# Six homes for the gathered expert rows, a gate matrix loaded in four pieces, and a re-dealt opening, in a two-layer block with 16,384 experts

## The chip, the cores and the metric

One core of one Trainium2 chip runs the whole program. The metric is the device time of one execution in microseconds (us); lower is better. The engines are named as the profile names them: PE (TensorE matmul), PEld (its weight load), DVE (VectorE), ACT (ScalarE), POOL (GpSimd) and SP (SyncE, which here only issues DMAs). The profile's granted clock is a share of the 2.4 GHz level; the other level is 1.2 GHz.

## What is computed

Two layers over 512 tokens (256 of `x`, 256 of `ctx`), width 1024. Each layer has a mixing half (a Hyena convolution whose filters come from a small sine network, a Fourier mix and differential attention) and a PEER half, in which each token takes 128 (8 heads of 16) of 16,384 experts. All of it is float32; only `x` of the last layer is returned. The parts that the change touches:

```python
def rms_norm(x, g):
    return x * lax.rsqrt(jnp.mean(x * x, axis=-1, keepdims=True) + EPS) * g
def modulate(x, g, shift, scale):
    return rms_norm(x, g) * (1 + scale) + shift

def hyena_kernels(L, w1, b1, freq, w2, b2, w3):      # does not depend on x
    h = jnp.sin(freq * (feats @ w1 + b1))
    h = jnp.sin(freq * (h @ w2 + b2))
    h = (h @ w3).reshape(L, 2, HY_ORDER, HY_WIDTH) * decay
    k = jnp.concatenate([h[:, 0], 0, h[:0:-1, 1]], axis=0)
    return jnp.fft.rfft(k / jnp.sum(jnp.abs(k), axis=0, keepdims=True), axis=0)

def peer(t, wq, keys, u, v):
    ...                                              # scores, top-k: idx, g  [T, 128]
    hid = jnp.einsum('td,tkd->tk', tc, u[ic])
    return jnp.einsum('tk,tkd->td', gc * gelu(hid), v[ic])
...
# per layer: shift, scale, gate, ... = silu(c) @ w_ada + b_ada   (6 x 1024 numbers per stream)
# mixing reads modulate(x, g_mix, shift, scale); PEER reads modulate of the result
```

## The kernel before

**Number form.** Matmuls are done as three float32r products: `split` (L106 on ACT, L110 on DVE) cuts a tile into a high part (`wh`, `vh`, `ah`) and the rest (`wl`, `vl`, `al`), and PE forms high*high, high*low, low*high (`mm`, L98; `mm3`). A weight chunk is 512 KB, loaded by `wraw` (L138 to L140) into the ring `w4` of six buffers. The instructions are put into an order for each engine by a scheduler, which follows the priorities of program order; `pin` keeps the marked DVE instructions in their written order.

**The opening** (`ada_first`, layer 0 only). `modulate` needs shift and scale of layer 0. For each of eight steps, one chunk of `w_ada` (a shift column block) is multiplied with `silu(c)` on DVE, two `scalar_tensor_tensor` (STT) with a sum into `mods` (L171) and one add of the bias each (L175); one chunk of `w_ada1` (rows of the scale matrix) goes through PE into two PSUM banks. In between `x` is loaded in four parts, squared on ACT, its squares are added on POOL (`tot`, L217), summed over partitions on PE, turned into 1/rms (`rs`, L220 and L221), and POOL multiplies `x` by `rs` (L200). At the end the scale row is transposed on PE (the small matmuls after L204), and `modulate` writes `nh` and `nl`, which every projection matmul (`pm<-nh,wh` ...) of phase 1 reads. Only behind `modulate` does the program write out `filters`: the sine network (tiles `sa`, `sk`), its product with the decay (`hd`), the sum of magnitudes (`ab`, L301), its reciprocal (`rn`, L305) and the transform with the matrix `fwd` into five tiles `K`. They are a generator, and a `drain` runs it at once.

**The experts.** All 16,384 experts are computed densely for 384 of layer 0's tokens: 128 blocks of 128 experts, two blocks to a superblock, so 64 superblocks in a loop. `stage1` of a block forms the hidden values `a` (1024 deep product, GELU), or for 32 blocks loads them from DRAM (`a<-Hd`, L796), where an earlier stage (`prefill`) left them. They are then multiplied by the gate matrix (`a<-a,gt`, L800, zero where a token didn't choose the expert) and split into `ah`, `al`. `stage2` of the superblock before loads its two `v` chunks (`wv`, L809, three buffers), splits them in four halves (`vh`, `vl`) and adds into six PSUM banks. The gate matrix of eight blocks (four superblocks, a *group*) is one load of 1.5 MB (`gt<-Gd`, L792). The two blocks of the first superblock of each of the 16 groups are prefilled ones. `a` has three buffers. Layer 1 runs the same loop for its 256 tokens, without the next part.

**The gathered rows.** The last 128 tokens of layer 0 don't go through the dense loop. Instead POOL fetches, for each of the 128 places k, one row of `u` for each token (`row<-in_ug_dram,ix`, L1049, 512 KB), and DVE forms its dot product with the token (L1067); four per superblock in the first 32 superblocks. In the second 32 superblocks the rows come from `v` and DVE adds them into `acc[:, 0:2]` (L1077, the first by L1075). These DVE instructions are pinned. A row tile has three buffers, so a gather waits on POOL's queue until DVE is done with the row three before it. Of `acc` (eight parts of 512 columns; the token vectors and the sum lie in the first two) parts 2 to 7 are not used in this stage.

## Time and profile before

| what | us |
| --- | --- |
| median of 3 runs | 3024.02 (3019.01 to 3027.01) |
| the profiled execution | 3018.95 |
| its span | 3017.2 |
| opening, up to the first projection matmul | 56.14 |
| phase 1 of layer 0 (with the filters) | 48.66 (56.14 to 104.80) |
| experts of layer 0 | 965 (887 to 1852) |
| experts of layer 1 | 621 (2387 to 3008) |

How to read it: the profiled execution lies 1.75 us above its own span and 5.07 us below the median. The page's busy times are means over stages with unlike limits, so the table is cut by stage: what a stage can give back is read from its waits and its granted clock. A row of a timeline gives start, duration, engine, line, operation, output<-inputs, the count where several stand in one row, and in brackets the idle time ahead of it with what ended that.

### The profile page before, as it was taken

How to read it: one execution, taken by the hardware profiler on the slowest of the kernel's cores; microseconds unless marked ns; L12 is line 12 of the kernel's file. 1: busy time of each engine (PE TensorE's matmuls, PEld its weight loads, DVE VectorE, ACT ScalarE, POOL GpSimd, SP SyncE). 2: the span in 40 equal slices, each digit the busy share in tenths (PEclk: the TensorE clock that was granted, in tenths of full speed). 3: DMA queues.
4: the chain of work that ended last, by engine and by line, in shares of the span. 5: the costliest groups of instructions: out<-in, count | busy, mean ns of one | idle time of the engine just before them, and what ended most of it. 6: DMA issues, size and time to landing. Idle time of an engine off the chain costs nothing.

```text
span 3017.2 us, 43660 instructions
## 1 busy us (share of the span) xinstructions
PE 2864.0 (95%) x15976; PEld 2435.9 (81%) x15976; DVE 2223.2 (74%) x4464; ACT 1247.6 (41%) x2294; POOL 700.7 (23%) x609
## 2 busy tenths in 40 slices
PE   6889999999989999999999999899799999999999
PEld 2678778776667888888898897788788898899888
DVE  7766786797977887888887787746688657765665
ACT  3334565421443333333333334336414455555554
POOL 4544433430013333333333332300200000000000
PEclk8899999999999999999999999999999999999999
DMA  7323555233788898889888885225457977766662
GB/s 261 108 97 116 175 180 220 101 114 105 278 332 326 315 326 300 307 318 323 312 317 300 307 312 186 81 97 176 165 162 250 331 249 243 259 223 223 221 224 103
DMA packets 234536, 682.19 MB, mean 226 GB/s; under 512 B 21956, under 2 KB 92682, under 8 KB 231120
## 3 DMA queue, kind: packets, MB, share of 16 engines
...
q8 instruction: 125, 2.05, 0.3%
...
HBM read 612.20 MB, written 67.11 MB: 225 GB/s over the span
## 4 chain that ended last, share of the span: by engine, by line
PE 52%; issue 15%; DVE 14%; DMA 13%; POOL 4%; ACT 2%; POOLq 0%; DVEq 0%; SPq 0%; ACTq 0%
PE pm L98 32%; PE pa L98 19%; DMA row<-in_ug_dram,ix 7%; DMA row<-in_v_dram,ix 4%; DVE og L734 3%; POOL row L1049 2%; DVE wl L110 1%; DVE oa L730 1%; DVE junk L171 1%; DVE acc L1077 1%; DVE junk L1067 1%; DVE vl L110 1%; POOL qt L466 0%; DMA a<-Hd 0%; POOL pr L167 0%
## 5 line engine op out<-in xcount | busy, mean ns | idle before, releaser
L98 PE MATMUL pm<-th,wh 128*128 128x256 f32 (+2 forms) x1680 | 532.4, 317 | 2.3 <-DVE th L241 2.3
L98 PE MATMUL pm<-tl,wh 128*128 128x256 f32 (+2 forms) x1680 | 530.2, 316 | 3.3 <-DVE tl L242 3.2
L98 PE MATMUL pm<-th,wl 128*128 128x256 f32 (+2 forms) x1680 | 529.7, 315 | 0.7 <-DVE wl L110 0.7
L106 ACT CAST wh<-w 128x1024 fp32r<-128x1024 f32 x328 | 343.0, 1047 | 409.3 <-PE pm L98 351.1
L110 DVE TENSOR_TENSOR wl<-w,wh 128x1024 fp32r<-128x1024 f32 x312 | 392.5, 1259 | 161.5 <-ACT wh L106 160.7
L98 PE MATMUL pa<-vl,ah 128*128 128x512 f32 x1024 | 406.1, 397 | 26.5 <-DVE vl L110 26.5
L110 DVE TENSOR_TENSOR vl<-wv,vh 128x512 fp32r<-128x512 f32 x512 | 339.1, 687 | 119.2 <-ACT vh L106 113.6
L106 ACT CAST vh<-wv 128x512 fp32r<-128x512 f32 x512 | 305.3, 619 | 265.4 <-PE pm L98 86.0
L98 PE MATMUL pa<-vh,ah 128*128 128x512 f32 x1024 | 402.5, 394 | 5.1 <-ACT vh L106 5.1
L98 PE MATMUL pa<-vh,al 128*128 128x512 f32 x1024 | 403.7, 394 | 0.3 <-DVE al L110 0.3
L98 PE MATMUL pm<-acc,w 128*128 128x256 f32 (+1 forms) x1280 | 355.6, 427 | 8.6 <-ACT acc L1011 8.6
L98 PEld LDWEIGHTS pm<-tl,wh 128*128 128x128 f32 x1680 | 320.9, 191 | 13.6 <-DVE tl L242 4.5
L98 PEld LDWEIGHTS pm<-th,wh 128*128 128x128 f32 x1680 | 321.0, 191 | 11.8 <-DVE th L241 2.9
L98 PEld LDWEIGHTS pm<-th,wl 128*128 128x128 f32 x1680 | 320.8, 191 | 5.4 <-DVE wl L110 0.9
L106 ACT CAST ah<-a 128x384 fp32r<-128x384 f32 (+1 forms) x256 | 117.7, 460 | 439.5 <-DVE a L800 399.6
L98 PEld LDWEIGHTS pm<-acc,w 128*128 128x128 f32 x1280 | 235.8, 191 | 78.0 <-ACT acc L1011 9.0
L1049 POOL DMA_INDIRECT row<-in_ug_dram,ix x128 | 165.3, 1291 | 507.7 <-DVE junk L1067 298.5
L98 PEld LDWEIGHTS pa<-vl,ah 128*128 128x128 f32 x1024 | 194.7, 190 | 70.5 <-DVE vl L110 32.7
L1049 POOL DMA_INDIRECT row<-in_v_dram,ix x128 | 170.6, 1332 | 311.5 <-DVE acc L1077 279.3
L98 PEld LDWEIGHTS pa<-vh,ah 128*128 128x128 f32 x1024 | 194.5, 190 | 44.8 <-ACT vh L106 6.3
L98 PEld LDWEIGHTS pa<-vh,al 128*128 128x128 f32 x1024 | 194.7, 190 | 41.1 <-DVE al L110 0.8
L1077 DVE SCALAR_TENSOR_TENSOR acc<-row,gg,acc 128x1024 f32<-128x1024 f32 x127 | 162.8, 1282 | 62.7 <-DMA row<-in_v_dram,ix 61.8
(309 smaller groups left out, 5292.5 us busy)
## 6 DMA issues: line engine op xcount, KB each, us to landing
w<-in_u_dram SPq DMA_DIRECT2D x256, 512.0 KB, 4.2
wv<-in_v_dram SPq DMA_DIRECT2D x256, 512.0 KB, 4.9
w<-in_w_ada_dram SPq DMA_DIRECT2D x96, 512.0 KB, 4.3
w<-in_w_in_dram SPq DMA_DIRECT2D x88, 512.0 KB, 3.8
...
w<-in_wq_dram SPq DMA_DIRECT2D x32, 512.0 KB, 3.6
...
```

What stands on the lines that cost most here:

```text
L98: T.matmul(o, l, r, start=start, stop=stop, skip_group_check=True)
L106: S.copy(hi, src)
L110: (eng or V).tensor_tensor(lo[:, ks], src[:, ks], hi[:, ks].bitcast(F32), ALU.subtract)
L171: i = V.scalar_tensor_tensor(slot((P, 1024), BF16, "junk"), w, 1.0, sil[:, s], op0=ALU.mult, op1=ALU.mult, accum_out=m)
L730: V.tensor_tensor(oa, row(0), iob, ALU.is_equal)
L734: V.tensor_tensor(og[:, w * HG:(w + 1) * HG], oa, gv[:, w * HG:(w + 1) * HG, None].to_broadcast([P, HG, P, 2]), ALU.mult)
L1049: nc.gpsimd.indirect_dma_start(out=r, out_offset=None, in_=src, in_offset=bass.IndirectOffsetOnAxis(ap=ix, axis=0))
L1067: pin(V.scalar_tensor_tensor(slot((P, 1024), BF16, "junk"), r, 1.0, ta, op0=ALU.mult, op1=ALU.mult, accum_out=hg[:, k:k + 1]))
L1077: pin(V.scalar_tensor_tensor(ta, r, gg[:, k:k + 1], ta, op0=ALU.mult, op1=ALU.add))
```

## The change

There are four parts. First, the rows with odd k are gathered into parts 2 to 7 of `acc`, three places in turn, and those with even k into the three buffers as before: six homes. Second, the gate matrix of a group is loaded in four pieces of 384 KB (three of the twelve column blocks each); the pieces of the next group are written one at a time into the even blocks of the current group, and those of the first group ahead of the loop. Third, `wv` gets four buffers in place of three, and the tiles `a`, `ah`, `al` are cut to the width that is used. Fourth, in the opening half of shift (four of eight column blocks) joins scale on PE: a step loads 1536 columns in two pieces (512 KB and 256 KB) and has three matmuls, and DVE does four chunks in place of eight. POOL's additions of squares and its multiplication by `rs` go to DVE. The generator `filters` is started ahead of the loop and moved on by one step behind every second chunk, and what is left of it, the five `K` steps, is drained behind `modulate`.

```diff
@@ -74,8 +74,8 @@
     def slot(shape=(P, 512), dt=F32, name="t"):
         return scope["sl"].tile(list(shape), dt, tag="sl", name=nm(name))
 
-    def tagged(tag, dt=F32, bufs=2):
-        return scope["ex"].tile([P, 512], dt, tag=tag, name=nm(tag), bufs=bufs)
+    def tagged(tag, dt=F32, bufs=2, n=512):
+        return scope["ex"].tile([P, n], dt, tag=tag, name=nm(tag), bufs=bufs)
 
     def b16t(shape=(P, 8, 512), dt=F32, name="b"):
         return b16.tile(list(shape), dt, tag="b16", name=nm(name))
@@ -174,7 +174,9 @@
                     pin(i)
                 V.tensor_tensor(m, m, b, ALU.add)
 
-    def ada_first(x, rs):
+    NSH = 4
+
+    def ada_first(x, rs, side):
         cT = slot((P, 8, 32), name="cT")
         V.memset(cT, 0.0)
         ct = slot((P, 8, 2), name="ct")
@@ -183,30 +185,41 @@
             nc.scalar.dma_start(sil[:, s], A["crow"][s:s + 1, :].to_broadcast([P, 1024]))
         S.activation(cT[:, :, 0:2], ct, AF.Silu)
         S.activation(sil, sil, AF.Silu)
-        ps = [pmt() for _ in range(2)]
+        next(side)
+        nb = (8 + NSH) // 4
+        ps = [pmt() for _ in range(nb)]
         tot = slot(name="tot")
         for c in range(8):
-            ada(0, c, c + 1)
-            w = wraw(A["w_ada1"][:, c])
-            for h in range(2):
-                mm(ps[h][0:32], cT[:, c], w[:, h * 512:(h + 1) * 512], c == 0, c == 7)
-            if c < 4:
-                nc.sync.dma_start(x[:, 2 * c:2 * c + 2], A["xT"][:, 2 * c:2 * c + 2])
-                for k in (2 * c, 2 * c + 1):
-                    squares(x, k, 0, NT, tot, eng=G)
-            if c == 4:
-                summed(tot, 0, NT, rs)
-                for k in range(8):
-                    G.tensor_tensor(x[:, k], x[:, k], rs, ALU.mult)
+            for a in range(0, nb * 512, 1024):
+                k = min(1024, nb * 512 - a)
+                w = w4.tile([P, 1024], F32, tag="w4", name=nm("w4"))
+                nc.sync.dma_start(w[:, :k], A["w_ada1"][:, c, a:a + k])
+                for q in range(k // 512):
+                    mm(ps[a // 512 + q][0:32], cT[:, c], w[:, q * 512:(q + 1) * 512], c == 0, c == 7)
+            if c % 2 == 0:
+                nc.sync.dma_start(x[:, c:c + 2], A["xT"][:, c:c + 2])
+                f = NSH + c // 2
+                if f < 8:
+                    ada(0, f, f + 1)
+            else:
+                for k in (c - 1, c):
+                    squares(x, k, 0, NT, tot)
+                next(side, None)
+        summed(tot, 0, NT, rs)
+        for k in range(8):
+            V.tensor_tensor(x[:, k], x[:, k], rs, ALU.mult)
         pt = pat()
-        for q in range(2):
+        for q in range(nb):
             m = slot(name="m1")
             (S.copy if q % 2 else V.tensor_copy)(m[0:32], ps[q][0:32])
             for f in range(4):
                 k = 4 * q + f
                 mm(pt[:, k * 32:(k + 1) * 32], m[0:32, f * P:(f + 1) * P], ident[0:32, 0:32], k == 0, True)
-        V.tensor_tensor(mods[:, 0, :, 8:16], pt[:, 0:256].rearrange("p (f s) -> p s f", s=32)[:, 0:2],
-                        pv(0, "b_ada")[:, None, 8:16].to_broadcast([P, 2, 8]), ALU.add)
+        p4 = pt.rearrange("p (f s) -> p s f", s=32)[:, 0:2]
+        for d, k in ((8, 0), (0, 8)):
+            w = min(8, 8 + NSH - k)
+            V.tensor_tensor(mods[:, 0, :, d:d + w], p4[:, :, k:k + w],
+                            pv(0, "b_ada")[:, None, d:d + w].to_broadcast([P, 2, w]), ALU.add)
 
     def squares(x, c, a, b, tot, new=slot, eng=None):
         if c == 0:
@@ -764,7 +777,7 @@
             for c in range(8):
                 cs = slice(c * P, (c + 1) * P)
                 mm3(ps[:, :n], uh[:, cs], ul[:, cs], th[:, c, :n], tl[:, c, :n], c == 0, c == 7)
-        a = scope["ha"].tile([P, 512], F32, tag="a", name=nm("a"))
+        a = scope["ha"].tile([P, NT - NG], F32, tag="a", name=nm("a"))
         S.activation(a[:, :n], ps[:, :n], AF.Gelu)
         return a
 
@@ -784,28 +797,37 @@
     def experts(l, n, npre, th, tl, Gd, Hd, acc, hook):
         nq = n // 32
         pacc = [pat() for _ in range(4)] + [pmt() for _ in range(n // P * 2 - 4)]
-        gt = [None]
+        gts = {}
+        pieces = 4
+
+        def gates(g, i):
+            if i == 0:
+                gts[g] = b16t((P, nq, GB, 32), name="gt")
+            qs = slice(i * nq // pieces, (i + 1) * nq // pieces)
+            nc.sync.dma_start(gts[g][:, qs], Gd[:, qs, g * GB:(g + 1) * GB, :])
+
+        for i in range(pieces):
+            gates(0, i)
 
         def stage1(b):
-            if b % GB == 0:
-                gt[0] = b16t((P, 16, GB, 32), name="gt")
-                nc.sync.dma_start(gt[0][:, :nq], Gd[:, :nq, b:b + GB, :])
+            if b % 2 == 0 and b // GB + 1 < P // GB:
+                gates(b // GB + 1, b % GB // 2)
             if b in PRE_BLOCK[l]:
                 k = PRE_BLOCK[l].index(b)
-                a = scope["ha"].tile([P, 512], F32, tag="a", name=nm("a"))
+                a = scope["ha"].tile([P, NT - NG], F32, tag="a", name=nm("a"))
                 nc.sync.dma_start(a[:, :n], Hd[k, :, :n])
             else:
                 a = hidden(l, n, b, th, tl)
             a3 = a[:, :n].rearrange("p (q k) -> p q k", k=32)
-            V.tensor_tensor(a3, a3, gt[0][:, :nq, b % GB], ALU.mult)
-            ah, al = tagged("ah", F32R, 4), tagged("al", F32R, 4)
+            V.tensor_tensor(a3, a3, gts[b // GB][:, :, b % GB], ALU.mult)
+            ah, al = tagged("ah", F32R, 4, n), tagged("al", F32R, 4, n)
             split(ah[:, :n], al[:, :n], a[:, :n])
             return ah, al
 
         def stage2(b0, blocks):
             ws = []
             for i in range(SB):
-                w = scope["ex"].tile([P, 1024], F32, tag="wv", name=nm("wv"), bufs=3)
+                w = scope["ex"].tile([P, 1024], F32, tag="wv", name=nm("wv"), bufs=4)
                 nc.sync.dma_start(w, A["v"][l, b0 + i])
                 ws.append(w)
             vs = {}
@@ -869,11 +891,13 @@
         fd = mp.tile([P, 2, P], F32, name=nm("fd"))
         rope = mp.tile([P, 2, 3, 64], F32, name=nm("rope"))
         pre = x is None
+        K = []
+        side = filters(l, fwd, K)
         if pre:
             x = b16t(name="x")
         rs = slot(name="rs")
         if pre:
-            ada_first(x, rs)
+            ada_first(x, rs, side)
         nc.gpsimd.dma_start(fwd, A["fwd"])
         nc.gpsimd.dma_start(inv, A["inv"])
         nc.gpsimd.dma_start(fd, A["fd"])
@@ -882,8 +906,7 @@
         nl = big.tile([P, 8, NT], F32R, tag="B", name=nm("nl"))
         gains(l, "g_mix", 1)
         modulate(l, x, rsl if last else None, 0, L if last else NT, 0, nh, nl)
-        K = []
-        drain(filters(l, fwd, K))
+        drain(side)
 
         br = b16t(name="br")
         vx = b16t(name="vx")
@@ -1044,8 +1067,11 @@
         drain(pf)
         pools(es, f"e{l}", ex=2, sl=1)
 
-        def rows_of(src, ix):
-            r = scope["ex"].tile([P, 1024], F32, tag="row", name=nm("row"), bufs=3)
+        def rows_of(src, ix, k):
+            if k % 2:
+                r = acc[:, 2 + k // 2 % 3 * 2:4 + k // 2 % 3 * 2].rearrange("p a b -> p (a b)")
+            else:
+                r = scope["ex"].tile([P, 1024], F32, tag="row", name=nm("row"), bufs=3)
             nc.gpsimd.indirect_dma_start(out=r, out_offset=None, in_=src,
                                          in_offset=bass.IndirectOffsetOnAxis(ap=ix, axis=0))
             return r
@@ -1063,14 +1089,14 @@
             ta = acc[:, 0:2].rearrange("p a b -> p (a b)")
             for k in range(4 * (sb % 32), 4 * (sb % 32) + 4):
                 if sb < 32:
-                    r = rows_of(A["ug"], ix[:, 0, k:k + 1])
+                    r = rows_of(A["ug"], ix[:, 0, k:k + 1], k)
                     pin(V.scalar_tensor_tensor(slot((P, 1024), BF16, "junk"), r, 1.0, ta, op0=ALU.mult,
                                                op1=ALU.mult, accum_out=hg[:, k:k + 1]))
                 else:
                     if k == 0:
                         S.activation(hg, hg, AF.Gelu)
                         V.tensor_tensor(gg, gg, hg, ALU.mult)
-                    r = rows_of(A["v"][0].rearrange("b p d -> (b p) d"), ix[:, 1, k:k + 1])
+                    r = rows_of(A["v"][0].rearrange("b p d -> (b p) d"), ix[:, 1, k:k + 1], k)
                     if k == 0:
                         V.tensor_scalar(ta, r, gg[:, k:k + 1], None, op0=ALU.mult)
                     else:
```

Two small hunks are left out: the result rows also take the ring of four `wv` buffers, and the host puts the columns of half of shift behind those of scale in `w_ada1`, which thereby holds 1536 columns.

Where the scheduler puts these instructions shows in their order on the engines. The first place is SP's queue at the start of a group of layer 0's experts, before (`w4` are `u` and `w_ada` chunks, `a<-Hd` the two prefilled blocks of the next superblock, `gt` the gate matrix):

```order
L809 DMA wv_1695_8456<-in_v_dram 128x1024
L796 DMA a_1654_8286<-Hd_974_4623 128x384
L796 DMA a_1657_8293<-Hd_974_4623 128x384
L140 DMA w4_1748_8684<-in_u_dram 128x1024
L792 DMA gt_1780_8832<-Gd_973_4622 128x12x256
L140 DMA w4_1755_8722<-in_u_dram 128x1024
L809 DMA wv_1696_8458<-in_v_dram 128x1024
L809 DMA wv_1727_8604<-in_v_dram 128x1024
```

and after:

```order
L831 DMA wv_1685_8457<-in_v_dram 128x1024
L818 DMA a_1645_8286<-Hd_972_4623 128x384
L818 DMA a_1648_8293<-Hd_972_4623 128x384
L140 DMA w4_1733_8681<-in_u_dram 128x1024
L807 DMA gt_1644_8284<-Gd_971_4622 128x3x256 x4
L140 DMA w4_1740_8719<-in_u_dram 128x1024
L831 DMA wv_1714_8602<-in_v_dram 128x1024
L831 DMA wv_1715_8604<-in_v_dram 128x1024
```

The four pieces stand together at the place of the one load, behind the two loads from `Hd` and one of `u`; both `wv` loads of a superblock now stand ahead of the `Hd` loads, where one of them stood behind the gate matrix and a load of `u`.

The second place is PE's queue in the second half of the opening, before (`pm` sums scale, `pa_52` takes the transposed scale, `pa_65` is the first matmul of the filters):

```order
L98 MATMUL pm_9_122<-w4_43_231,cT_7_114 32x512
L98 MATMUL pm_10_123<-w4_43_231,cT_7_114 32x512
L98 MATMUL pm_9_122<-w4_47_243,cT_7_114 32x512
L98 MATMUL pm_10_123<-w4_47_243,cT_7_114 32x512
L98 MATMUL pm_9_122<-w4_51_255,cT_7_114 32x512
L98 MATMUL pm_10_123<-w4_51_255,cT_7_114 32x512
L98 MATMUL pa_52_259<-ident_78,m1_53_260 128x32 x4
L98 MATMUL pa_52_259<-ident_78,m1_54_266 128x32 x4
L98 MATMUL pa_65_329<-feats_57_313,w1_58_315 64x256
```

and after (`pm_20` to `pm_22` sum scale and half of shift, `pa_32` is the second sine layer, `pa_45` and `pa_48` its product with `w3`):

```order
L98 MATMUL pm_21_151<-w4_40_209,cT_7_114 32x512
L98 MATMUL pa_32_181<-sa_18_140,w2_11_126 64x256
L98 MATMUL pm_22_152<-w4_41_213,cT_7_114 32x512
L98 MATMUL pm_20_150<-w4_51_236,cT_7_114 32x512
L98 MATMUL pm_21_151<-w4_51_236,cT_7_114 32x512
L98 MATMUL pm_22_152<-w4_52_240,cT_7_114 32x512
L98 MATMUL pm_20_150<-w4_56_252,cT_7_114 32x512
L98 MATMUL pa_45_223<-w3_13_130,sa_33_183 128x512
L98 MATMUL pa_48_229<-w3_14_131,sa_33_183 128x512
```

The filters' first matmuls now stand between those of the weight chunks, and a matmul of a later chunk waits in the queue behind one of the filters; the ten `K` matmuls follow behind the scale's, still ahead of the first projection matmul.

The third place is DVE's queue at the end of the opening, before:

```order
L204 COPY m1_53_260<-pm_9_122 32x512
L175 TENSOR_TENSOR mods_92<-mods_92,par_91 128x1
L110 TENSOR_TENSOR wl_102_425<-w4_100_422,wh_101_424 128x1024
L208 TENSOR_TENSOR mods_92<-pa_52_259,par_91 128x2x8
L230 SCALAR_TENSOR_TENSOR ngain_93<-mods_92,par_91 128x8 x2
L269 TENSOR_SCALAR sa_66_331<-pa_65_329,hp_60_319 64x256
L270 TENSOR_SCALAR sk_67_332<-sa_66_331 64x256
L241 CAST nh_55_277<-x_5_112 128x512
L271 TENSOR_SCALAR sk_67_332<-sk_67_332 64x256
L242 TENSOR_TENSOR nl_56_278<-x_5_112,nh_55_277 128x512
```

and after (`rn` and `rs` are the two reciprocals, `K` two of the filters' transforms):

```order
L110 TENSOR_TENSOR wl_100_425<-w4_98_422,wh_99_424 128x1024
L318 RECIPROCAL rn_75_309<-pa_44_222 128x512
L234 RECIPROCAL rs_6_113<-rs_6_113 128x512
L214 COPY m1_80_330<-pm_20_150 32x512
L210 TENSOR_TENSOR x_5_112<-x_5_112,rs_6_113 128x512 x8
L214 COPY m1_82_342<-pm_22_152 32x512
L335 TENSOR_TENSOR K_86_393<-pa_85_390,rn_75_309 128x512
L110 TENSOR_TENSOR wl_111_477<-w4_109_474,wh_110_476 128x1024
L221 TENSOR_TENSOR mods_92<-pa_79_329,par_91 128x2x8
L221 TENSOR_TENSOR mods_92<-pa_79_329,par_91 128x2x4
L243 SCALAR_TENSOR_TENSOR ngain_93<-mods_92,par_91 128x8 x2
```

Between the last weight chunk and `nh` DVE now has the two reciprocals, the eight multiplications of `x` and the first `K` tiles; the sine steps, which stood between the `nh` and `nl` rows, have gone ahead of this piece.

## Rows read from the trace of the kernel before

**Rows 1.** Windows by stage: window, its length, each engine's busy time, PEclk, DMA share, GB/s.
```profile
0.00:56.14 56.14, 27.12 (x53) 7.91 (x53) 39.45 (x61) 13.47 (x19) 37.12 (x42) 0.80 0.83 312
56.14:104.80 48.66, 46.07 (x154) 29.01 (x154) 35.58 (x60) 21.45 (x40) 19.64 (x19) 0.95 0.26 82
104.80:113.13 8.33, 1.40 (x12) 1.15 (x11) 8.33 (x14) 3.20 (x8) 3.89 (x7) 0.74 0.29 86
...
887.00:1852.00 965.00, 934.10 (x4560) 832.92 (x4561) 774.19 (x1163) 343.12 (x579) 332.42 (x254) 0.98 0.88 311
...
2387.00:3008.00 621.00, 620.66 (x3796) 558.79 (x3795) 390.83 (x649) 315.92 (x569) 0.00 (x0) 1.00 0.65 225
```

**Rows 2.** Waits in 887 to 1852: what waited for what, total us, times, longest.
```profile
POOL row L1049 <- DVE junk L1067: 301.0, 95, 21.9
...
DVE junk L1067 <- DMA row<-in_ug_dram,ix: 66.9, 38, 4.3
DVE acc L1077 <- DMA row<-in_v_dram,ix: 61.8, 43, 3.9
...
DVE a L800 <- DMA a<-Hd: 34.1, 16, 16.1
...
PE pa L98 <- DVE vl L110: 26.5, 14, 4.2
```

**Rows 3.** Waits of SP in the same stretch, in the same columns.
```profile
SPq L796 <- DVE al L110: 36.9, 14, 4.1
```

**Rows 4.** Waits of PE in layer 1's experts, 2387 to 3008: all there are.
```profile
PE pa L98 <- DVE al L110: 0.3, 1, 0.3
```

**Rows 5.** Timeline of SP at two group starts.
```profile
1056.95 2.03 SPq L796 DMA_DIRECT2D a<-Hd  x2
...
1176.60 4.14 SPq L796 DMA_DIRECT2D a<-Hd  x2
```

**Rows 6.** Timeline of DVE and PE at the second of these group starts.
```profile
1178.68 1.23 DVE L1067 SCALAR_TENSOR_TENSOR junk<-row,acc 128x1024 bf16<-128x1024 f32 x1 [2.02 <-DMA row<-in_ug_dram,ix]
...
1186.17 0.56 DVE L800 TENSOR_TENSOR a<-a,gt 128x384 f32<-128x384 f32 x1 [1.91 <-DMA a<-Hd]
...
1187.38 0.79 PE L98 MATMUL pa<-vl,ah 128*128 128x512 f32 x1 [3.72 <-DVE vl L110]
```

**Rows 7.** DMA issues in 887 to 1852: count, KB each, median us to landing.
```profile
a<-Hd SPq DMA_DIRECT2D x30, 192.0 KB, 6.0
...
row<-in_ug_dram,ix POOLq DMA_INDIRECT x125, 6.5
```

**Rows 8.** The chain of waits that ended last, through the opening.
```profile
34.68 3.35 DVE rs L221
...
49.99 4.67 PE pa L98 x18
```

**Rows 9.** Groups of DVE, 10 to 60: busy, mean ns, idle time before.
```profile
L171 DVE SCALAR_TENSOR_TENSOR junk<-w,sil 128x1024 bf16<-128x1024 f32 x16 | 24.6, 1554 | 11.5 <-ACT sil L185 10.4 <-DMA w<-in_w_ada_dram 1.1
...
L242 DVE TENSOR_TENSOR nl<-x,nh 128x512 fp32r<-128x512 f32 x3 | 2.0, 673 | 0.0
...
L273 DVE SCALAR_TENSOR_TENSOR sa<-sk,sa 64x256 f32<-64x256 f32 x3 | 1.2, 407 | 0.0
```

**Rows 10.** Timeline of PE: the filters among the projection matmuls.
```profile
72.08 3.70 PE L98 MATMUL pa<-w,sa 64*128 64x512 f32 x8
...
80.09 1.13 PE L98 MATMUL pa<-ab,ones 128*128 128x512 f32 x2 [1.32 <-POOL ab L301]
...
83.79 4.06 PE L98 MATMUL pa<-hd,fwd 128*128 128x512 f32 x8 [0.96 <-POOL hd L310]
...
91.12 1.88 PE L98 MATMUL pa<-hd,fwd 128*128 128x512 f32 x4
```

**Rows 11.** DMA issues, 0 to 60, in the columns of rows 7.
```profile
w<-in_w_ada_dram SPq DMA_DIRECT2D x19, 512.0 KB, 8.3
...
dec<-in_decay_dram POOLq DMA_DIRECT2D x2, 256.0 KB, 3.3
```

6 lines of the change are left out of this document (3 added, 3 removed).

## The prediction

> **What bounds the kernel now.** I read the windows by stage first. They cut the span into places where PE is the bound and places where it waits. In layer 1's experts PE is busy for 620.66 of 621 us at full clock [rows 1]: nothing is to be had there but fewer matmuls, and the change leaves their number alone. In layer 0's experts PE is busy for 934.10 of 965 us and its mean clock is 0.98 [rows 1]: 30.9 us idle, and about 0.02 x 965 = 19 us lost to the lower clock behind the gaps. In the opening PE does almost nothing of use, and no projection matmul can start for 56.14 us [rows 1]; the eight us behind phase 1 belong to DVE, which is busy in all of them while PE has 1.40 us of work [rows 1].
>
> Then the waits of layer 0's experts. PE waits 14 times, 26.5 us in all, for `vl` [rows 2]. Layer 1 runs the same loop with the same loads of gates and hidden values, without gathers, and its PE waits once, 0.3 us [rows 4]. So the gaps come with the gathers. DVE waits 66.9 + 61.8 = 128.7 us for gathered rows, since POOL can't issue a gather before DVE is done with the row three before it (301.0 us of such waits in the first half alone) [rows 2]. Those DVE instructions are pinned, and `al` and `vl` stand behind them.
>
> Why that reaches PE only at group starts, the timelines show. Two blocks are then loaded from `Hd`, and the second load needs an `a` buffer that the `al` of an earlier block frees; SP waits for that 14 times, 36.9 us in all [rows 3]. At a clean start the two loads take 2.03 us, at a bad one 4.14 us [rows 5]. At the bad one DVE has lost 2.02 us to a row, then 1.91 us to `Hd`, and PE stands for 3.72 us [rows 6].
>
> **The change part by part.** *Six homes.* A gather now waits for the row six before it, one and a half superblocks. A superblock is 965 / 64 = 15 us, so about 22 us are left for a gather that lands in 6.5 us [rows 7]; with three homes it was 11 us on an even spread, and less where the four rows stand close. I take it that nearly all of the 128.7 us of DVE's waits go. Most of that was DVE's own slack (774.19 of 965 us busy [rows 1]); what counts is the group starts. There 26.5 us of PE's gaps [rows 2] and, of the 19 us of clock, those behind these gaps can go, which I put at 16: 42.5 in all, 44 with what little rounds it. It does not all go: the second `Hd` load still waits for an `al`, and `Hd` still lands in 6.0 us [rows 7]. I take three quarters, **-32 us**, with bounds of -12 and -44. The 16.1 us that DVE waits at the stage's own start [rows 2] stay. Next behind that is PE itself.
>
> *Gates in four pieces.* In SP's queue the four pieces stand at the place of the one load. Three more issues of at most 1 us each (two `Hd` issues take 2.03 [rows 5]) stand ahead of loads that serve a later superblock, some 15 us on. Layer 1 shows that one load of this kind costs nothing at this place [rows 4]. **0**, bounds -2 and +5. The fourth `wv` buffer and the narrower tiles: both `v` loads of a superblock now stand ahead of the two `Hd` loads in SP's queue, where one stood behind them; a late `v` load reaches PE through `vl`, and PE's waits for `vl` are all counted already [rows 2]. **0** beside the 32.
>
> *Filters out of phase 1.* All 24 of their larger matmuls now stand ahead of the first projection matmul. In phase 1 they and their waits take 3.70, 1.13 + 1.32, and from 83.79 - 0.96 to 91.12 + 1.88 another 10.2 us [rows 10]: 16.4, less the overlap of modelled ends, **-16 us** on PE, which phase 1 is bound by (46.07 of 48.66 us [rows 1]).
>
> *A longer opening.* Bytes loaded by the step loop stay (16 x 512 KB before; 4 and 8 x 512 KB and 8 x 256 KB now). DVE loses eight of sixteen products with `silu(c)`, 1.55 us each [rows 9] = -12.4. It gains seven additions of squares, eight multiplications by `rs` and four `hd`, 19 x 0.67 [rows 9] = +12.8; the second reciprocal, +3.35 [rows 8]; the second half of the first sine and the second sine, some ten instructions of at most 0.41 [rows 9] = +4. That is about +8 on an engine that was busy for 39.45 of 56.14 us [rows 1], so packed tight it would end where it does now, and POOL, which did these sums more slowly, is out of the way: from there a little below nothing, -3. But DVE will not be packed. Each filter step passes from PE to DVE to ACT and back, PE's matmuls of the next chunk stand behind that in its queue, and the ring of six gives the next loads their buffers only behind those matmuls. One load there lands 8.3 us after its issue [rows 11]. I expect one such landing to be laid bare, and about 1 us beside it: **+9 us**; with two, +17. The first projection matmul then comes at about 65 us.
>
> *Behind phase 1.* DVE has less to do in phase 1, so part of the 8.33 us stretch in which it runs alone [rows 1] goes: **-3 us**, bounds 0 and -8.
>
> Sum: -32 + 0 - 16 + 9 - 3 = **-42 us**. It is made against the profiled execution, 3018.95 us, which gives 2977; the median of before lies 5.07 us above that execution, and I keep that distance: 3024.02 - 42 = **2982 us**.
>
> A rule of the Trainium skill speaks against the smaller loads: "DMA: Bandwidth & Descriptors", section "Anatomy of one DMA", gives each DMA a fixed part of about 2.0 us beside its bytes, and the section "Bandwidth" asks for 1 MiB and more a DMA. By that, the four additional loads of the opening would cost 4 x 2.0 = 8 us (an estimate from that page) and the sum would be -34. In the trace a 256 KB load took 3.3 us and 512 KB loads among many took 8.3 [rows 11], so the fixed part is there for one load, but many are in flight at a time, and the opening moved 312 GB/s on the mean [rows 1]; I leave the sum as it is, and rival A is what the rule would make of it.
>
> **The rivals.** *A: the opening gives back all that the filters give.* The `w_ada1` pieces wait for ring buffers one behind another, so the four additional loads don't overlap: 4 x 3.3 = +13 us [rows 11] on top of +9, and the gain behind phase 1 is lost as well, since DVE is then late everywhere. Opening +22 - 16 = +6, experts -32: 3024 - 26 = **2998**. For it: a 512 KB load took 8.3 us there [rows 11], so one that starts late is felt. Against it: the DMA engines are busy for 0.83 of that stretch [rows 1], so loads overlap. The rule above points here.
>
> *B: the group starts stay.* The second `Hd` load is late because of `al` and the load's own landing, not because of rows; the four gate pieces then go out as one burst just as before. Only a quarter of the 42.5 goes, -12 with the rest of the row waits: 3024 - 12 - 10 = **3002**. For it: at the bad start 1.91 us of `Hd` stand beside 2.02 of rows [rows 6]. Against it: clean starts have the same loads [rows 5], and layer 1 has no gap at all [rows 4]. Both A and B: -12 + 6 = **3018**.
>
> *C, slower: six gathers crowd the loads.* With up to six 512 KB gathers in flight, 3 MB, the DMA engines (0.88 busy at 311 GB/s [rows 1]) serve POOL's queue first and the `Hd` loads land late. What the homes win at a bad start is 4.14 - 2.03 = 2.1 us of SP's issue [rows 5]; so this decides from a landing of 6.0 + 2.1 = 8.1 us on. At 10 us, 1.9 us at each of 15 starts are lost anew, +28, less 10 of the opening: **3042**. Against it: the number of bytes is the same, and gathers ahead of need leave the average demand as it is.
>
> **How the numbers follow.** The forecast 2982 has 0.54, A 0.17, B 0.14, both 0.07, C 0.08. About 0.3%, 9 us, is what a measurement of this kernel can tell from no change. Forecast, A and B are faster by more: 0.85. Both together, -6, is within it: 0.07. C is slower: 0.08. By its own bounds the forecast reaches from 3024 - 44 - 16 - 3 - 8 = 2953 to 3024 - 12 - 16 + 17 + 5 = 3018, though not all terms end on one side at once. A range of **2958 to 3008** holds the middle of that with A and B, and leaves out both-together, C and the ends.
>
> **What would show it.** Homes: DVE's waits for gathered rows under 20 us in place of 128.7, PE's wait for `vl` under 8 us in place of 26.5, the clock of the stage at 0.99 or more, and the stage some 32 us shorter. If rows are never waited for and PE's gaps stay, B holds. If `a<-Hd` lands in 8 us or more, C. Opening: the first projection matmul at about 65 us (72 and above: A), no `K`, `hd` or `sa` matmul behind it, phase 1 about 33 us long. Layer 1's experts stay at 621 us; if they move, the narrower tiles or the gate pieces did what I put at nothing. The prediction is wrong in its main term if the gaps at group starts don't come from the gathers.

## The result, and the profile after

The changed kernel takes **2989.08 us** (median of four runs, 2988.32 to 2991.12) where the kernel before takes 3024.14 in the same comparison: a ratio of 0.9887, 95% interval 0.987 to 0.9904. A second comparison gave 2989.13 against 3024.52 (0.9885, 0.9867 to 0.9903). Forecast were 2982 us and a range of 2958 to 3008; the gain is 35 us where 42 were forecast. One of the five runs of a kernel below (filters behind modulate) took 10011.31 us and is left out of its ratio. The profiled execution took 2988.38 us, its span 2986.5.

Where it came from shows best at marks on PE. The names are used from here on: *first projection* (the first `pm<-nh,wh`), *phase 1 end* (the end of the last of its 144 projection matmuls, `pm<-nh,wh` and the like), *qr* (the first transposition of the attention's queries), and the first and last `pa<-vh,ah` of layer 0's experts.

| us | before | changed | difference of the stretch |
| --- | --- | --- | --- |
| first projection | 56.14 | 79.20 | +23.1 |
| phase 1 end | 121.17 | 112.44 | -31.8 |
| qr | 164.84 | 155.51 | -0.6 |
| first matmul of the experts | 890.50 | 886.76 | +5.6 |
| last matmul of the experts | 1848.62 | 1819.42 | -25.5 |
| end of the span | 3017.17 | 2986.48 | -1.5 |

The profiled executions differ by 30.6 us and the medians by 35, since the profiled run of before (3018.95) lies at the fast end of its runs; the parts below are parts of the 30.6.

The windows of the changed kernel by these marks, in the columns of [rows 1]; the last answers to the experts' row there:

```profile
0.00:79.20 79.20, 51.79 (x108) 17.04 (x109) 48.17 (x79) 20.71 (x32) 24.69 (x37) 0.83 0.70 244
79.20:112.44 33.24, 33.24 (x148) 27.35 (x147) 32.34 (x63) 17.23 (x35) 12.42 (x12) 1.00 0.35 114
112.44:155.51 43.07, 35.20 (x251) 30.99 (x251) 37.92 (x51) 17.96 (x37) 27.18 (x22) 0.95 0.43 147
887.00:1822.00 935.00, 923.53 (x4557) 825.64 (x4558) 773.16 (x1158) 355.04 (x575) 352.93 (x251) 1.00 0.88 317
```

The window named phase 1 ahead of the prediction ended at 104.80, where 22 of the 144 matmuls were still to come; by the mark used here it took 65.0 us. (The `K` matmuls, which the order ahead of the prediction counts as ten, are twenty.) It now takes 33.2 us, all of them PE's, at full clock, and the experts run at a clock of 1.00 where they had 0.98. The waits in the experts, against [rows 2]:

```profile
DVE a L822 <- DMA a<-Hd: 37.2, 20, 3.7
...
PE pa L98 <- DVE vl L110: 11.2, 10, 2.8
...
DVE acc L1103 <- DMA acc<-in_v_dram,ix: 6.0, 2, 5.0
...
DVE junk L1093 <- DMA acc<-in_ug_dram,ix: 1.8, 1, 1.8
```

DVE's waits for gathered rows have shrunk from 128.7 us to 7.8. PE's wait for `vl` has shrunk from 26.5 to 11.2 us, all of it at ten group starts, and DVE's wait for `Hd` inside the stage has grown: 37.2 us, where 34.1 - 16.1 = 18.0 lay behind the start before. SP's wait for the buffer of an `Hd` load, against [rows 3]:

```profile
SPq L818 <- DVE al L110: 13.2, 10, 2.3
```

And the wait of PE at the stage's start, 4.1 us before (the longest of its waits for `vh`). The first gate matrices, hidden values, `v` chunks and gathers are all loaded there at once; the homes alone already show 7.1 us at this place, so the longer wait is theirs and not the gate pieces':

```profile
PE pa L98 <- ACT vh L106: 7.3, 1, 7.3
```

### The profile page after: what moved, and what is told of

It reads as the page before. It is cut to its first block, busy times and chain, and to the rows that moved or that the text cites. A ratio compares the mean times of both kernels' runs of the same rounds, so it can differ in the third digit from the quotient of the medians.

```text
span 2986.5 us, 43845 instructions
## 1 busy us (share of the span) xinstructions
PE 2852.1 (96%) x16000; PEld 2425.5 (81%) x16000; DVE 2225.1 (75%) x4457; ACT 1263.9 (42%) x2293; POOL 698.4 (23%) x594
## 4 chain that ended last, share of the span: by engine, by line
PE 72%; DVE 13%; issue 5%; DMA 5%; POOL 3%; ACT 2%; SPq 0%; POOLq 0%; DVEq 0%; ACTq 0%
PE pm L98 45%; PE pa L98 26%; DVE og L747 3%; DMA a<-Hd 2%; DVE wl L110 1%; DVE oa L743 1%; DVE junk L171 1%; POOL pr L167 1%; DMA w<-in_w_ada_dram 1%; DMA Hd<-a 1%; DMA w<-in_u_dram 1%; POOL qt L479 1%; DVE junk L1093 1%; DVE ob L744 0%; DVE vl L110 0%
## 5 line engine op out<-in xcount | busy, mean ns | idle before, releaser
L110 DVE TENSOR_TENSOR vl<-wv,vh 128x512 fp32r<-128x512 f32 x512 | 346.4, 689 | 148.6 <-ACT vh L106 143.5
L106 ACT CAST vh<-wv 128x512 fp32r<-128x512 f32 x512 | 316.5, 622 | 298.1 <-PE pm L98 172.2
L98 PE MATMUL pa<-vl,ah 128*128 128x512 f32 x1024 | 402.1, 393 | 11.2 <-DVE vl L110 11.2
L98 PEld LDWEIGHTS pa<-vl,ah 128*128 128x128 f32 x1024 | 192.7, 188 | 53.9 <-DVE vl L110 16.6
L98 PEld LDWEIGHTS pa<-vh,ah 128*128 128x128 f32 x1024 | 193.0, 189 | 46.1 <-ACT vh L106 8.4
L1075 POOL DMA_INDIRECT row<-in_ug_dram,ix x64 | 93.5, 1461 | 433.1 <-DVE junk L1093 237.0
L781 ACT ACTIVATE a<-pm 128x384 f32<-128x384 f32 (+1 forms) x256 | 110.9, 433 | 146.5 <-PE pm L98 144.9
L822 DVE TENSOR_TENSOR a<-a,gt 128x384 f32<-128x384 f32 (+1 forms) x256 | 122.8, 486 | 65.6 <-DMA a<-Hd 59.7
```

What stands on the lines that cost most here:

```text
L98: T.matmul(o, l, r, start=start, stop=stop, skip_group_check=True)
L106: S.copy(hi, src)
L110: (eng or V).tensor_tensor(lo[:, ks], src[:, ks], hi[:, ks].bitcast(F32), ALU.subtract)
L781: S.activation(a[:, :n], ps[:, :n], AF.Gelu)
L822: V.tensor_tensor(a3, a3, gts[b // GB][:, :, b % GB], ALU.mult)
L1075: nc.gpsimd.indirect_dma_start(out=r, out_offset=None, in_=src, in_offset=bass.IndirectOffsetOnAxis(ap=ix, axis=0))
```

## The experiments

All times of stages are from the profiled execution of each kernel, by the marks above. "Experts" is the stretch from their first to their last matmul: 958.1 us before, 932.7 in the changed kernel. Each ratio is against runs of the kernel before taken beside that kernel; their medians lie between 3020.4 and 3026.4 us, so kernels measured at different times are compared by their ratios.

| kernel | ratio to before (95%) | first projection | qr | experts |
| --- | --- | --- | --- | --- |
| changed | 0.9887 (0.987 to 0.9904) | 79.2 | 155.5 | 932.7 |
| changed, second time | 0.9885 (0.9867 to 0.9903) | 81.1 | 157.4 | 936.2 |
| homes alone | 0.9911 (0.9878 to 0.9944) | 56.2 | 164.2 | 938.4 |
| gates and v buffers alone | 0.9977 (0.996 to 0.9993) | 56.1 | 164.5 | 966.9 |
| opening alone | 0.996 (0.9943 to 0.9977) | 77.8 | 154.1 | 966.9 |
| changed without the new opening | 0.992 (0.9898 to 0.9941) | 56.2 | 166.6 | 938.6 |
| changed, filters behind modulate | 0.9932 (0.9909 to 0.9955) | 58.4 | 172.0 | 935.8 |
| changed, sine one step later | one run, 2984.83 us | 67.3 | 149.6 | 936.6 |
| changed, x early | one run, 2992.65 us | 80.5 | 154.1 | 937.4 |
| changed, x early and sine later | 0.989 (0.9869 to 0.9911) | 66.9 | 152.5 | 935.5 |
| changed, K late | one run, 2998.53 us | 79.9 | 157.2 | 936.9 |
| changed, four a buffers | 0.9906 (0.9887 to 0.9925) | 77.7 | 154.0 | 931.1 |
| changed, sine later and four a buffers | 0.9881 (0.986 to 0.9901) | 66.5 | 148.5 | 932.7 |

**Homes alone.** Into the kernel before, only this:

```diff
-        def rows_of(src, ix):
-            r = scope["ex"].tile([P, 1024], F32, tag="row", name=nm("row"), bufs=3)
+        def rows_of(src, ix, k):
+            if k % 2:
+                r = acc[:, 2 + k // 2 % 3 * 2:4 + k // 2 % 3 * 2].rearrange("p a b -> p (a b)")
+            else:
+                r = scope["ex"].tile([P, 1024], F32, tag="row", name=nm("row"), bufs=3)
```

> The kernel before with the six homes alone. Layer 0's experts, from their first matmul to their last, took 958.1 us before and 932.7 in the changed kernel. Theory H (the homes do it): DVE's waits for rows nearly gone (under 20 us of 128.7), the stage at 930 to 938 us, the whole about 3024 - 23 = 3001 us. Rival G (the gate pieces and the order of the v loads do it): the waits for rows go all the same, but PE's wait for vl stays at 20 us or more and the stage at 948 or more, the whole at 3014 or more.

Measured: 2994.23 us, experts 938.4. H holds: the waits are gone, the stage ends 0.4 us above its 930 to 938, and the whole is 7 us better than its 3001. DVE's waits and the landings in this kernel (waits: total us, times, longest; landings as in [rows 7]):

```profile
DVE a L800 <- DMA a<-Hd: 43.9, 23, 4.5
...
DVE acc L1080 <- DMA acc<-in_v_dram,ix: 5.7, 1, 5.7
...
DVE junk L1070 <- DMA acc<-in_ug_dram,ix: 1.0, 1, 1.0
```
```profile
a<-Hd SPq DMA_DIRECT2D x30, 192.0 KB, 7.5
...
row<-in_ug_dram,ix POOLq DMA_INDIRECT x61, 7.2
```

Rows are hardly waited for any more (6.7 us), but both kinds of load land later than in [rows 7]: gathers 7.2 us after their issue (6.5 before), `Hd` 7.5 (6.0). That is the late landing of rival C, short of the 8.1 us from which it would have eaten the gain; DVE's longer wait for `Hd`, 43.9 us in this kernel, goes with it.

**Gates and v buffers alone** (pieces of the gate matrix, the fourth `wv` buffer, narrow tiles; three row buffers). Into the kernel before:

```diff
+            nc.sync.dma_start(gts[g][:, qs], Gd[:, qs, g * GB:(g + 1) * GB, :])
...
-                nc.sync.dma_start(gt[0][:, :nq], Gd[:, :nq, b:b + GB, :])
...
-                w = scope["ex"].tile([P, 1024], F32, tag="wv", name=nm("wv"), bufs=3)
+                w = scope["ex"].tile([P, 1024], F32, tag="wv", name=nm("wv"), bufs=4)
```

> The kernel before with the gate pieces, the fourth v buffer and the narrower tiles alone; rows have three homes. H: nothing or little, the stage at 952 to 960 us, the whole at 3018 to 3026. G: the second v load ahead of the Hd loads and smaller gate loads shorten the group starts without any new home, the stage at 945 us or less, the whole at 3012 or less. Layer 1's experts stay within 2 us of 621 in both.

Measured: ratio 0.9977, but the profiled run was at the slow end of its ten (3026.8; they reach from 3008.25), and in it nothing has moved:

```profile
DVE junk L1076 <- DMA row<-in_ug_dram,ix: 72.4, 41, 4.1
DVE acc L1086 <- DMA row<-in_v_dram,ix: 66.0, 43, 3.7
...
PE pa L98 <- DVE vl L110: 25.5, 14, 3.9
```

The waits for rows and PE's wait for `vl` are those of [rows 2]. G is refuted: it asked for a stage of 945 us or less and a whole of 3012 or less. Its experts took 966.9 us, and so did those of the next kernel, whose expert code is that of before: with three homes the stage differs by 9 us from profile to profile (before had 958.1, and 19 runs of it in this comparison reach from 3014.3 to 3032.0). The ratio (7 us) is clear of 1, but where these 7 us lie can't be read from one profile, and a slow one; this stays open.

**Opening alone.** Into the kernel before, the new `ada_first`, the started generator and the wider `w_ada1`; the experts as before.

```diff
+        K = []
+        side = filters(l, fwd, K)
...
-            ada_first(x, rs)
+            ada_first(x, rs, side)
...
-        drain(filters(l, fwd, K))
+        drain(side)
```

> The kernel before with the new opening alone. In the changed kernel the first projection matmul came at 79.2 us (56.1 before), the first attention transposition (qr) at 155.5 (164.8), but the experts began only 3.7 us earlier. If the opening is a part by itself: first projection matmul at 78 to 81, experts 3 to 5 us earlier, the whole at 3017 to 3022 us, experts at 958 as before. Rival: the experts' start is late because of the homes or gate pieces, not because of the opening; then the experts begin 7 us or more earlier and the whole is at 3014 to 3017.

Measured: 3013.38 us, 13 less. Its window up to the first projection:

```profile
0.00:77.77 77.77, 50.22 (x109) 16.82 (x109) 48.16 (x79) 20.72 (x32) 24.66 (x37) 0.82 0.72 248
```

First projection at 77.8 as in the changed kernel, and the experts begin at 879.2, which is 11.3 us ahead of before and 7.5 ahead of the changed kernel. So the rival holds (the whole came out just under its 3014): part of the opening's gain is spent at the experts' start, and by the homes. From the first prefill matmul to the first of the experts the kernels with three homes need 307.4 to 308.6 us, those with six 311.4 to 312.0. Another part is a spread that no run here explains: from qr to the prefill, whose code is the same in all, before needed 417.1 us, homes alone 411.1 and `x` early with the sine later 421.1.

**Changed, filters behind modulate.**

```diff
         S.activation(sil, sil, AF.Silu)
-        next(side)
...
-                next(side, None)
```

> The changed kernel with the filters drained behind modulate again, and all else of the new opening left. It tells what the interleaving is worth. Theory I (the interleaved filters are what makes the opening 23 us longer: the first product with silu(c) waits 10 us for the first sine, a reciprocal stands ahead of rs, matmuls of K stand between the transposes of scale): first projection matmul at 55 to 62 us, phase 1 16 us longer on PE again, and the whole within 6 us of the changed kernel's 2989. Rival X (x loaded over eight steps and its sums on DVE make it longer): first projection matmul still at 68 or later, and the whole 8 us or more above the changed kernel.

Measured: 3006.45 us. This is the run that taught most. The first projection comes at 58.4, as theory I has it, and yet qr comes 16.5 us later than in the changed kernel, and by the ratios the whole is 14 us slower, where theory I allowed 6:

```profile
58.37:111.84 53.47, 50.81 (x178) 34.35 (x179) 40.67 (x65) 20.65 (x39) 21.49 (x21) 0.95 0.23 74
111.84:171.99 60.15, 37.51 (x252) 32.97 (x251) 45.42 (x74) 22.49 (x45) 28.62 (x24) 0.80 0.37 123
```
```profile
PE pm L98 <- ACT wh L106: 13.1, 1, 13.1
PE pm L98 <- DVE wl L110: 8.2, 1, 8.2
...
ACT pr L168 <- POOL pr L167: 19.2, 10, 8.6
```

Phase 1 takes 53.5 us in place of 33.2, with the filters' matmuls back in it, and behind it PE waits 13.1 us for `wh` and 8.2 for `wl`. DVE now has all of the filters to do behind the first projection and is busy without a pause from 111.84 to 137. ACT is not short of time: its splits `wh` stand behind sums (`pr`, for the later columns of `w_ada`) that wait for POOL, 19.2 us in all from 92 to 140, and others that wait for DVE. So the splits come late. The rest of the new opening (half of shift on PE, the sums of squares and the scaling of `x` on DVE) is by itself worth less than nothing at this mark: qr at 172.0 against 164.8 before. The interleaving carries the opening's gain, though it delays the first projection by 20.8 us.

**Changed, sine one step later.**

```diff
         S.activation(sil, sil, AF.Silu)
-        next(side)
```

> The changed kernel, but the filters start one step later: the first sine layer is written behind the second weight chunk and not ahead of the first, every later step moves with it, and one more step is left for behind modulate. Marks of the changed kernel: first product with silu(c) on DVE at 21.7 us, first projection matmul at 79.2, first attention transposition (qr) at 155.5; with the filters behind modulate 58.4 and 172.0. Theory S (the first sine, which waits on PE behind the second chunk's load, holds DVE and with it the buffers of the weight ring): the first product at 12 to 15 us, first projection matmul at 64 to 70, qr at 140 to 146. Theory X (what holds it is that the four parts of x are loaded over eight steps, so that rs comes at 59 in place of 35): first projection matmul at 76 or later, qr at 152 or later.

In the changed kernel the first sine's matmul on PE (`pa<-feats,w`), DVE's first steps behind it, and DVE's two reciprocals are these:

```profile
17.99 1.81 PE L98 MATMUL pm<-w,cT 128*32 128x512 f32 x2 [3.06 <-DMA w<-in_w_ada_dram]
19.73 1.11 PE L98 MATMUL pa<-feats,w 33*64 33x256 f32 x2
...
20.88 0.53 DVE L282 TENSOR_SCALAR sa<-pa,hp 64x256 f32<-64x256 f32 x1 [10.12 <-PE pa L98]
...
21.66 1.21 DVE L171 SCALAR_TENSOR_TENSOR junk<-w,sil 128x1024 bf16<-128x1024 f32 x1
...
55.99 3.35 DVE L318 RECIPROCAL rn<-pa 128x512 f32<-128x512 f32 x1
59.26 3.29 DVE L234 RECIPROCAL rs<-rs 128x512 f32<-128x512 f32 x1
```

DVE stands 10.12 us for the first sine's matmul, which in PE's queue is behind matmuls whose weight load lands at 17.99; only then come the products. The last matmuls of the weight chunks, and the first copy of the scale row (`m`), come here:

```profile
43.19 5.34 PE L98 MATMUL pm<-w,cT 128*32 128x512 f32 x12
...
62.47 0.62 DVE L214 COPY m<-pm 32x512 f32<-32x512 f32 x1
```

With the sine later these places are:

```profile
16.03 1.22 DVE L171 SCALAR_TENSOR_TENSOR junk<-w,sil 128x1024 bf16<-128x1024 f32 x1 [14.21 <-DMA w<-in_w_ada_dram]
...
45.66 2.76 PE L98 MATMUL pm<-w,cT 128*32 128x512 f32 x6
...
48.97 1.27 DVE L213 COPY m<-pm 32x512 f32<-32x512 f32 x2
```

S says that the sine's wait costs DVE's time and with it the buffers of the weight ring. The first product now starts when its load lands, at 16.03 and not at 12 to 15. But the last weight chunk is done at the same time in these two profiles (48.53 and 48.42; over all profiles of the interleaved opening at 48.2 to 53.9 with the sine first and at 46.1 to 48.4 with it later), so the ring is not what makes their difference. DVE itself is: its copy of the scale row comes 13.5 us earlier, ahead of both reciprocals. The edit moves more than the first sine: `rs` now stands ahead of `rn`, and no `K` matmul between the parts of scale, so the run shows what the later start of all the filters is worth and not the sine's wait alone. The windows up to qr:

```profile
0.00:67.31 67.31, 46.32 (x104) 13.87 (x105) 41.91 (x73) 21.14 (x33) 21.78 (x37) 0.92 0.77 273
67.31:110.39 43.08, 38.02 (x152) 29.43 (x151) 39.47 (x75) 17.80 (x36) 13.32 (x16) 0.92 0.39 124
110.39:149.63 39.24, 34.93 (x252) 30.92 (x251) 34.10 (x45) 16.95 (x35) 25.04 (x19) 0.98 0.45 147
```

S holds for the first projection (79.2 to 67.3), but it expected too much at qr, which gains 5.9 and not 10 to 15: phase 1 grows from 33.2 to 43.1 us, since the last `K` matmuls now stand in it and PE waits there for a PSUM buffer that a `K` on DVE gives back only behind all of `nh` and `nl`:

```profile
PE pa L98 <- DVE K L334: 5.1, 1, 5.1
```

**Changed, x early; and both.** `x` is loaded and squared in the first four steps and scaled behind the fifth, as before but on DVE:

```diff
+            if c < 4:
+                nc.sync.dma_start(x[:, 2 * c:2 * c + 2], A["xT"][:, 2 * c:2 * c + 2])
+                for k in (2 * c, 2 * c + 1):
+                    squares(x, k, 0, NT, tot)
+            if c == 4:
+                summed(tot, 0, NT, rs)
+                for k in range(8):
+                    V.tensor_tensor(x[:, k], x[:, k], rs, ALU.mult)
             if c % 2 == 0:
-                nc.sync.dma_start(x[:, c:c + 2], A["xT"][:, c:c + 2])
                 f = NSH + c // 2
...
-                for k in (c - 1, c):
-                    squares(x, k, 0, NT, tot)
...
-        summed(tot, 0, NT, rs)
```

> The changed kernel with x loaded, squared and scaled as before in the first four steps (on DVE), the filters in the same steps as in the changed kernel. X: rs at 40 us or earlier, first projection matmul at 66 or earlier, qr at 143 or earlier. S: DVE still begins at 20 us or later, the last weight chunk comes as late as now, first projection matmul at 72 or later and qr at 148 or later.

> The changed kernel with both: x in the first four steps and the first sine one step later. If S and X are the two causes and add up: first projection matmul at 56 to 62 us, qr at 133 to 140, which is 15 to 22 us ahead of the changed kernel; the whole at 2967 to 2976 us where the changed kernel has 2989. If the time then is lost again to DVE's backlog behind phase 1: qr at 148 or later, the whole at 2982 or more.

`x` early alone moves `rs` from 59.3 to 41.3 us and the first projection not at all (80.5), because DVE still begins late, and its copy of the scale row comes only at 64.76, behind its last products and `rn`:

```profile
21.30 0.54 DVE L284 TENSOR_SCALAR sa<-pa,hp 64x256 f32<-64x256 f32 x1 [11.56 <-PE pa L98]
```

X is refuted as the cause. With both, the first projection comes at 66.9, and qr at 152.5:

```profile
66.92:110.56 43.64, 43.64 (x166) 32.16 (x167) 39.96 (x74) 18.95 (x38) 11.23 (x12) 0.95 0.27 87
110.56:152.45 41.89, 35.21 (x252) 31.00 (x251) 36.74 (x48) 17.12 (x35) 27.20 (x22) 0.97 0.44 150
```

PE is busy through all 43.6 us of phase 1, with 166 matmuls in it where the changed kernel has 148: the twenty `K` matmuls stand in it again. The whole is the changed kernel's (2988.86). Of the two outcomes that had been written down, the marks of the second came (qr at 148 or later, the whole at 2982 or more), but not by its cause: what was gained ahead of phase 1 was paid inside it, on PE, and not by DVE's backlog behind it.

**Changed, K late.**

```diff
         modulate(l, x, rsl if last else None, 0, L if last else NT, 0, nh, nl)
-        drain(side)
...
                 more_ada(ADA_EARLY)
+            if g == 0:
+                drain(side)
```

> The changed kernel with the reciprocal rn, the K steps and all that the filters have left moved from behind modulate to behind the first group of projections. In the changed kernel matmuls of K took 6.7 us on PE between the two halves of the transposed scale, and rn 3.35 us on DVE ahead of rs. Theory K (these stand in front of modulate): first projection matmul at 66 to 71 us, but 10 to 13 us of K matmuls then lie in phase 1, so qr moves by no more than 5 us from 155.5. If qr falls below 148, moving them out of the opening is a gain and not an exchange.

In the changed kernel PE's last stretch ahead of the first projection reads:

```profile
63.23 3.59 PE L98 MATMUL pa<-ident,m 32*128 32x32 f32 x16 [7.18 <-DVE m L214]
66.75 6.67 PE L98 MATMUL pa<-hd,fwd 128*128 128x512 f32 x8
...
74.35 3.70 PE L98 MATMUL pa<-df,fwd 128*128 128x512 f32 x8
77.89 1.88 PE L98 MATMUL pa<-hd,fwd 128*128 128x512 f32 x4
```

The wait for the row of scale, then matmuls of `K` between its transpositions (sixteen, then eight at 73.34) and behind them. The edit did not remove them: in PE's order sixteen of the twenty `K` matmuls stayed where they were, and on DVE `rn` still stood ahead of `rs`. PE's rows at the same place, and phase 1:

```profile
70.33 5.53 PE L98 MATMUL pa<-hd,fwd 128*128 128x512 f32 x8
75.79 1.07 PE L98 MATMUL pa<-ident,m 32*128 32x32 f32 x8
76.79 3.70 PE L98 MATMUL pa<-df,fwd 128*128 128x512 f32 x8
```
```profile
79.93:118.84 38.91, 36.92 (x152) 28.92 (x151) 35.16 (x65) 20.23 (x41) 13.60 (x16) 0.96 0.34 109
```

Only the last four matmuls and their `K` went behind the first group, phase 1 grew by 5.7 us, to 38.9, and PE waited there for a `K` on DVE (2.0 us). So this run shows that the later place is no gain for what did move; theory K itself was not tested and stays open.

**Changed, four a buffers** (`ha=4` in place of `ha=3`).

> The changed kernel with four buffers in place of three for the tiles a (they are 384 wide now, so the room is the same as for three of 512). The order on SP is unchanged. In the changed kernel SP still waits 13.2 us, 10 times, for an al that frees the buffer of an Hd load, and PE waits 11.2 us, 10 times, for vl at group starts. Theory R (the release of a buffer is what is left at group starts): SP's wait falls under 3 us, PE's wait for vl under 5, layer 0's experts from 932.7 to 925 to 929 us. Theory L (what is left is that the Hd loads land 6 us and more after their issue behind a u load, among gathers): SP's wait goes all the same, PE's wait stays at 8 to 12, the stage within 3 us of 932.7.

A group start of the changed kernel, SP's and DVE's rows:

```profile
1101.03 1.04 SPq L818 DMA_DIRECT2D a<-Hd  x2
...
1108.47 1.03 DVE L822 TENSOR_TENSOR a<-a,gt 128x384 f32<-128x384 f32 x2 [3.69 <-DMA a<-Hd]
```

The two loads are issued within 1.04 us, and DVE still waits 3.69 us for them. With four buffers SP waits for no `al` at an `Hd` load any more, and the rest stays:

```profile
DVE a L822 <- DMA a<-Hd: 34.7, 19, 4.5
...
PE pa L98 <- DVE vl L110: 10.1, 10, 2.6
```

Theory L holds: the release of a buffer is not what is left at group starts; the landing of `Hd` is what DVE still waits for there. The whole was 2992.86, no better.

**Changed, sine later and four a buffers; changed without the new opening; the changed kernel again.**

> The changed kernel with the filters one step later in the opening and four buffers for a. The later step alone moved qr from 155.5 to 149.6 us and gave 2984.83 in one run where the changed kernel had 2988.38. By theory S alone: 2983 to 2986 us, about 4 us under the changed kernel of the same call; with R another 4 to 8 less; if the 6 us at qr are lost to what follows, the same as the changed kernel.

> The changed kernel with the opening of before: homes, gate pieces and v buffers together. The homes alone had layer 0's experts at 938.4 us and the whole at 2994.2 on another chip. If the gate pieces and v buffers help only once the rows are out of the way: the stage at 931 to 935 us and the whole 3 to 6 us below homes alone, ratio 0.989 to 0.990. If they give nothing in any company: stage at 937 to 940, ratio 0.991. In both, the whole lies 6 to 10 us above the changed kernel, which is what the opening is worth at qr (155.5 against 164.8).

> The changed kernel itself, unaltered, beside the next three on one chip. Its first comparison gave 2989 against 3024, a ratio of 0.9887. If the parts add up, the sum of the parts measured apart (homes 0.9911, gates and v buffers 0.9977, opening 0.996) is 0.985; if they overlap, it stays at 0.987 to 0.990, the more so as the experts' stage of the kernel before varies from run to run.

The first gave 2988.85 us beside the changed kernel's 2989.13: the same. It reached the experts 7.2 us ahead of the changed kernel's second profile, and lost it again in layer 1's mixing half, which took 311.9 us from its first projection to its own prefill where the changed kernel took 305.7 and 303.4. Four buffers alone show that too (311.6), and the twelve profiles with three buffers lie between 301.2 and 306.8: the fourth buffer costs there what it may save elsewhere, for a reason that no run shows. No variant beat the changed kernel by more than the measurement can tell. The sine later without the fourth buffer was not measured again; its one run of 2984.83 stands beside a median of 3020.39 of the kernel before, which is the changed kernel's ratio too.

The second, all of the experts' part with the old opening, gave 2998.98 us and experts of 938.6, the time of homes alone; PE's wait for `vl` there is 14.1 us. So gate pieces and `v` buffers show nothing in the stage and add nothing to the homes; alone their ratio of 0.9977 stays unexplained. The opening is worth 2998.98 - 2989.13 = 9.9 us beside the homes. The parts measured alone come to 0.985, the whole to 0.9885, some 10 us less; but the intervals of the parts together are about as wide as that, so an overlap is likely and not shown.

## Why the prediction came out right, point by point

*Six homes, -32.* Measured -25.5 in the stage between the two profiles, and about +3 at its start. Three profiles with three homes have 958.1, 966.9 and 966.9 us, two of the changed kernel 932.7 and 936.2; by their means it is 964.0 - 934.4 = -29.6. The mechanism is right, and homes alone show it: the waits for rows went as forecast (7.8 us, under 20), and the stage got shorter with them. The size is near, a little under. PE still waits 11.2 us at ten group starts where under 8 were expected, and there DVE waits for `Hd`, which lands later beside the homes (7.5 us against 6.0). Rival C had named that late landing, and its own threshold of 8.1 us told rightly that it would not decide; that the landing is what keeps the rest of the gaps fits the run with four buffers, but no run changes it by itself. Rival B is refuted: more than half of PE's wait went. The clock, 1.00, met the 0.99 or more that was expected.

*Gates in four pieces, fourth `v` buffer, narrow tiles, 0.* Nothing that a stage shows; 0.2% in a comparison by themselves, and nothing on top of the homes. Layer 1's experts took 620.97 us from first to last matmul (2357.10 to 2978.07) against 620.25 before.

*Filters out of phase 1, -16, and behind phase 1, -3.* Together phase 1 and the way to qr lost 31.8 + 0.6 = 32.4 us where 19 were forecast. The filters' share was near: with the other parts of the opening changed and the filters back behind modulate, phase 1 takes 20.2 us more. (Of the filters' matmuls from their product with `w3` on there are 30, not 24; the sum of 16.4 us is read from rows and holds.) The term behind phase 1 was mis-sized. The whole 8.33 us stretch is gone, not 3 us of it, and that was its bound; what had not been counted is what lay around it, the matmuls at a granted clock of 0.50, the 1.2 GHz level, at the start of phase 1 and behind the stretch, in which PE had 1.40 us of work [rows 1]:

```profile
56.14:60.00 3.86, 3.85 (x8) 2.46 (x9) 3.86 (x10) 3.86 (x9) 0.07 (x1) 0.50 0.45 149
113.13:118.84 5.71, 5.71 (x13) 4.47 (x14) 5.71 (x5) 3.67 (x6) 5.71 (x4) 0.50 0.44 154
```

The changed kernel's phase 1 shows a clock of 1.00 and no wait. That it is 33 us long, as forecast, is luck: the forecast took 16 from a window of 48.66 us that left out 22 of its matmuls.

*A longer opening, +9.* It became +23.1, well past the +17 that was its bound. In the kernel before PE's last weight chunk and its first transposition of scale are these:

```profile
33.85 8.79 PE L98 MATMUL pm<-w,cT 128*32 128x512 f32 x16
...
49.99 3.62 PE L98 MATMUL pa<-ident,m 32*128 32x32 f32 x16 [7.34 <-DVE m L204]
```

With the rows of the experiments above, the 23.1 are three parts. The last chunk ends at 48.53 in place of 42.64: +5.9, less than the one landing (8.3 + 1) that was priced. From there to the first transposition it takes 14.7 us in place of 7.4: +7.3. From there to the first projection it takes 16.0 in place of 6.2: +9.8. The last two parts are the step that failed. The forecast put DVE's +8 into its idle time, but DVE stood 10.12 us for the first sine, and from 39.6 on it was the bound, without a pause, with `rn` and `rs` ahead of the scale row:

```profile
39.60:68.49 28.89, 17.36 (x42) 7.25 (x41) 28.89 (x32) 9.77 (x14) 15.82 (x10) 0.72 0.53 181
```

And it had all `K` matmuls ahead of the first projection, with no price for them there: the twenty take 6.67 + 3.70 + 1.88 = 12.3 us on PE among and behind the transpositions. With the sine one step later, which also moves some of these, the first projection comes at 67.3, +11.2. (The "-3" that the forecast works out for DVE packed tight does not enter its +9.) By the mark named in the prediction (72 and above) rival A would have been confirmed, and its result did not come: its mark was the wrong one.

These terms are one sum, and it came out: +23.1 - 31.8 - 0.6 = -9.3 at qr against +9 - 16 - 3 = -10. Two errors of 14 and 13 us cancelled. In part they are one and the same: work that stands ahead of the first projection doesn't stand behind it. With the filters behind modulate it is -20.8 at the first projection and +16.5 at qr, with `x` early and the sine later -12.3 and -3.1. In part it is luck: the wait for the first sine is not work, and with the sine later half of what the first projection gains (11.9) is left at qr (5.9). Between qr and the experts the changed kernel lost 5.6 us, which no term had: 3.2 of them from the prefill to the experts' start, where the homes' longer wait stands.
